# Turning the delta rule's outputs in 32 x 32 blocks on VectorE and placing the blocks by four loads, in a hybrid decoder layer

## The chip, the core and the metric

The kernel runs on one core of a Trainium2 chip. The metric is the device time of one execution in microseconds (us); lower is better. The program is built once, and its instructions stand in a fixed order on each engine: TensorE (PE), VectorE (DVE), ScalarE (ACT), GpSimd (POOL), and SyncE (SP), which issues most of the DMAs.

## What is computed

One decoder layer on 1024 tokens of 1024 features, in float32. After an RMS norm, one projection feeds two groups of four heads each: differential attention (group A) and a gated delta rule in chunks (group B). Their outputs are put side by side, projected, added to the input, and a squared-ReLU MLP of width 4096 follows.

```python
h = rms_norm(x, norm1_w); proj = h @ w_in
da_o = diff_attention(rms_norm(da_q), rms_norm(da_k), da_v, lam)      # 4 heads, values of 128
da_o = rms_norm(da_o, da_out_norm_w) * (1.0 - lam_init)
dn_o = gated_delta_rule(l2(conv_silu(q)), l2(conv_silu(k)), conv_silu(v), g, beta)
dn_o = rms_norm(dn_o, dn_out_norm_w) * silu(dn_z)                     # 4 heads of 128
x = x + concatenate([da_o, dn_o]) @ w_out
x = x + square(relu(rms_norm(x, norm2_w) @ w_up)) @ w_down
```

## The kernel before

Every large product is three matmuls of float32r parts: `hH` and `hL` hold the rounded value and the rest of the normed input, features on the partitions and tokens along the row. The order on TensorE is written out ahead of time by a planner, the class `Interleave` (L39): each stream of work is a generator with a priority, `flow.pe(ns)` moves the planned time on, `flow.chain(...)` gives the planned end of a chain on other engines, and `flow.hold(bank, t)` keeps a PSUM bank from being claimed before time t. The other engines' instructions are put in order by the framework's scheduler. The planner's times only set the order; on the chip every instruction waits for its own inputs.

The change lies between about 250 and 625 us, where these streams share TensorE:

- `scan` (L912) walks the eight chunks of 128 tokens of the delta rule. Its loads are `pka` (L920). `scan_out` (L966) makes a chunk's outputs: it loads `pkb` (L970) and `zgt` (L972), runs two sets of four matmuls (L980, L987), squares and sums on ScalarE (L994), and then a `scalar_tensor_tensor` for each head (L999) leaves the normed and gated rows, tokens on the partitions, in `oc`. GpSimd's queue stores them to `mixn_d` in DRAM (L1001).
- `da_units` (L1051) computes the queries, keys and values of the attention, two heads at a time (L1077 to L1079, 24 matmuls for one tile of 128 tokens). These matmuls are also what the planner fills gaps with. A finished tile of queries or keys goes on the list `late` with a due time; `da_turns` (L1030) takes it from there, turns it by two TensorE transposes (L1038, L1039) in a PSUM bank of the pool `px`, splits it and stores it to `qk_d` (L1044).
- `scores` (L1151) and `values` (L1232) are the attention, row of 128 queries by row, in the order head 0, head 1, and then heads 2 and 3 by turns from the last rows to the first. `scores` loads the keys `KS` (L1128) and the queries (L1143, L1144), multiplies (L1203, L1204), takes the maximum on VectorE (L1214) and the exponential on ScalarE (L1215). `values` turns the weights on TensorE (L1248, copied by L1250), multiplies by the values (L1260) into the bank `po`, copies the result to `om` (L1269), squares it into another part of the same bank (L1270) and scales it (L1274). Rows of heads 0 and 1 are stored to `mixa_d` by GpSimd's queue (L1276); for heads 2 and 3 the rows of one tile lie in `rows_of[tb]`, into whose first half the two stored heads are loaded (L1241).
- `mix_loads` (L1297) loads a stored tile of the delta rule's outputs into `mt` (L1305). `mixed` (L1308) calls `turn` (L1288) and through it `to_hT` (L293): four TensorE transposes into a `px` bank (L298), a rounding copy to `hH` (L303, ScalarE) and the rest to `hL` (L304, VectorE). It does so twice for each tile: for the four heads of the delta rule (`mt`) and for the four of the attention (`mx`).
- `outproj` (L1335) is the output projection from `hH` and `hL` (`half`, L1350 to L1352), followed for each tile by `norm2` (L1363): squares on ScalarE (L1370), the scale on VectorE (L1377) or ScalarE and GpSimd (L1379, L1380). `backs` (L1479) then turns the normed rows on TensorE (L298 for the first four tiles, which also keep a copy, L302; L1456 for the others).

The pool `px` has two PSUM banks for the query and key turns, the weights' turns, the `po` products and the `mixed` turns. SyncE's DMAs carry one of eight semaphores in rotation, so each also waits for the landing of the DMA eight places ahead of it. The MLP follows from 625 us to the end.

Of the kernel before, what the change touches and what calls it, by code (L numbers as in the profile page):

```python
# [18 lines left out]
P = 128  # L19
# [14 lines left out]
MIX_T = 5000.0  # L34
DMA_T = 2500.0
# [76 lines left out]
def vec(n, extra=0.0):  # L112
    return "V", 68.0 + 1.045 * n + extra
# [7 lines left out]
def tile_hymba_layer(  # L121
# [171 lines left out]
    def to_hT(src, tb, bank, k0=0, nk=KB, keep=None):  # L293
        sl = slice(tb * P, (tb + 1) * P)
        for g in range(0, nk, 4):
            ps = bank()
            for j in range(4):
                T.transpose(ps[:, j * P:(j + 1) * P], src[:, (g + j) * P:(g + j + 1) * P], ident)  # L298
            psv = ps.rearrange("p (k t) -> p k t", k=4)
            ks = slice(k0 + g, k0 + g + 4)  # L300
            if keep is not None:
                S.copy(keep, psv)  # L302
            S.copy(hH[:, ks, sl], psv)  # L303
            V.tensor_tensor(hL[:, ks, sl], psv, hH[:, ks, sl].bitcast(F32), ALU.subtract)  # L304
# [406 lines left out]

    def cols4(t, h, hf):
        return t[:, 8 * h + 4 * hf:8 * h + 4 * hf + 4]
# [252 lines left out]
    def scan_out(c, Sold, yy):  # L966
# [31 lines left out]
        for h in range(HEADS):  # L998
            V.scalar_tensor_tensor(oc[:, h * P:(h + 1) * P], oc[:, h * P:(h + 1) * P], f[:, h:h + 1],  # L999
                                   zgt[:, h * P:(h + 1) * P], ALU.mult, ALU.mult)  # L1000
# [4 lines left out]
        flow.chain(*[act(P, True)] * 4, vec(4), powr(4), vec(4), *[vec(P, 60)] * 4, start=t)  # L1005
# [45 lines left out]
    def da_units():  # L1051
# [12 lines left out]
        for i, (g, kind) in enumerate(todo):  # L1064
            (wh, wl), wt = w
            for j in range(NT):
# [17 lines left out]
                while len(late) > 2:  # L1084
                    yield flow.now + 50, None
# [7 lines left out]
                else:  # L1093
# [12 lines left out]
                    t = flow.chain(vec(4), powr(4), vec(256), start=t - flow.HOP)  # L1106
# [44 lines left out]
    def scores():  # L1151
        heads, npe, nsc = {}, 0, 0
        while state["da"] < 1:
            yield flow.now + 300, None
        heads[0] = load_head(0, ap), load_v(0, ap)
        q = load_q(*order[0])
        yield state["da_t"] + 3000, None
# [74 lines left out]
    def values():  # L1232
        for _ in order:
# [3 lines left out]
            if h == 2:  # L1237
                while "ax" not in pools or len(rows_of) + len([x for x in loads if not x[3]]) > 1:
                    yield flow.now + 50, None
                rows_of[tb] = pools["ax"].tile([P, 512], F32, tag="mx", name="mx", bufs=2)  # L1240
                nc.sync.dma_start(rows_of[tb][:, 0:256], mixa_d[tb])  # L1241
# [25 lines left out]
            sq = po[:, P:2 * P]  # L1267
# [6 lines left out]
            V.scalar_tensor_tensor(om, om, f, dawb, ALU.mult, ALU.mult)  # L1274
            if h < 2:
                nc.gpsimd.dma_start(mixa_d[tb, :, h * P:(h + 1) * P], om)  # L1276
            flow.pe((tb + 1) * MM)
            t = flow.chain(act(P))
            flow.hold(r, t)
# [6 lines left out]
    landed, hns = {}, {}  # L1286

# [9 lines left out]
    def mix_loads():  # L1297
        while not (pre and state["scan"]):
            yield flow.now + 200, None
        for i, t in enumerate(tiles):  # L1300
            while i >= 2 + state["mixed"]:
                yield flow.now + 50, None
            mt = pools["a2"].tile([P, 512], F32, tag="mt", name="mt", bufs=2)
            with tc.issue_after(newest["SP"].ins):
                nc.sync.dma_start(mt, mixn_d[t])  # L1305
            loads.append((mt, flow.now + MIX_T, t, 4))

    def mixed():  # L1308
        for i in range(2 * NT):
# [3 lines left out]
            x = min((x for x in loads if x[2] in over), key=lambda x: x[1])  # L1313
            r = yield from flow.bank("px")
            loads.remove(x)
            turn(r, *x)
            state["mixed"] += x[3] == 4
# [17 lines left out]
    def outproj():  # L1335
# [27 lines left out]
        def norm2(tb, pos):  # L1363
# [5 lines left out]
            for i in range(2):  # L1369
                S.activation(hn[i], accs[tb][:, 512 * i:512 * i + 512], AF.Square, accum_out=ss[:, i:i + 1])  # L1370
# [557 lines left out]
```

## Time and profile before

| | |
|---|---|
| median of 3 runs | 1233.85 us (1232.64 to 1236.31) |
| profiled execution: its own time | 1233.5 us |
| profiled execution: span from first to last instruction | 1231.8 us |
| granted TensorE clock, mean | 0.998 |
| PE busy | 1215.3 us, 99% |
| DVE busy | 829.9 us, 67% |
| ACT busy | 624.3 us, 51% |
| POOL busy | 151.3 us, 12% |

A row of a group reads: line, engine, operation, out<-in and shapes, count | busy us, mean ns of one | idle us of the engine before them and what ended it. In the list of waits, "PE a L1 <- DMA b: 2.8, 1, 2.8" says that PE stood idle ahead of line 1 until a transfer landed: in total, how often, and the longest. A view of one line gives durations as min/median/max in ns, and under a line that issues DMAs the time from issue to landing in us. In the timeline a row begins with its start in us and its length. A line number belongs to the kernel that the profile is of.

### The profile page before, as it was taken

The page shows a single profiled execution, that of the slowest core. Times are in us where ns is not written, and L with a number is a line of the kernel's source. Part 1 is how long each engine was busy: PE and PEld are TensorE (multiplying, and loading weights), DVE is VectorE, ACT ScalarE, POOL GpSimd, SP SyncE. Part 2 cuts the span into 40 slices and gives each one's busy share as a digit, 9 for nine tenths or more (in the row PEclk, how much of TensorE's full clock was granted, in tenths as well). Part 3 has the DMA queues.
Part 4 walks back from the last instruction along what each step waited for, and adds up shares of the span by engine and source line. Part 5 has one row for each costly group of instructions (what it writes and reads, how often), then busy time and mean ns, then how long its engine had stood idle before and what let it go on. Part 6 is the DMA issues. An engine that isn't in the chain of part 4 may idle for free.

```text
span 1231.8 us, 18793 instructions
## 1 busy us (share of the span) xinstructions
PE 1215.3 (99%) x6791; PEld 1052.0 (85%) x6791; DVE 829.9 (67%) x1534; ACT 624.3 (51%) x1249; POOL 151.3 (12%) x215
## 2 busy tenths in 40 slices
PE   9999999998999999999999999999999999999998
PEld 8978888898999998888888888888888888888886
DVE  6868797665647657776799544565569755777543
ACT  6587553344356555566766544454564333333330
POOL 2411110033434421001200000000000000000000
PEclk9999999999999999999999999999999999999999
DMA  9334654378648855223437433444479655423401
GB/s 351 103 111 119 167 163 86 78 244 240 223 146 246 241 162 159 84 74 109 157 120 257 171 129 145 171 171 154 154 244 386 229 178 184 162 103 103 137 35 69
DMA packets 155973, 202.12 MB, mean 164 GB/s; under 512 B 37688, under 2 KB 110952, under 8 KB 155880
## 3 DMA queue, kind: packets, MB, share of 16 engines
q1 hardware_dynamic: 151256, 187.28, 46.9%
q0 software_dynamic: 4480, 13.64, 2.9%
q8 instruction: 54, 0.88, 0.3%
q14 instruction: 39, 0.32, 0.1%
q10 hardware_dynamic: 144, 0.00, 0.0%
HBM read 135.86 MB, written 65.01 MB: 163 GB/s over the span
## 4 chain that ended last, share of the span: by engine, by line
PE 90%; DMA 3%; DVE 2%; ACT 2%; issue 1%; SPq 1%; POOL 1%; DVEq 0%; ACTq 0%; POOLq 0%
PE X L1527 5%; PE X L1526 5%; PE X L1525 5%; PE X L1825 4%; PE X L1823 4%; PE X L1824 4%; PE ps_dn L265 3%; PE ps_dn L267 3%; PE ps_dn L266 3%; PE ps_qk L1077 3%; PE ps_qk L1079 3%; PE ps_qk L1078 3%; PE Y L1525 3%; PE Y L1526 3%; PE Y L1527 3%; PE ps_o L1260 2%
## 5 line engine op out<-in xcount | busy, mean ns | idle before, releaser
L1443 ACT CAST hH<-ur 128x1024 fp32r<-128x1024 f32 x56 | 58.9, 1051 | 173.4 <-PE Y L1824 89.4
L1444 DVE TENSOR_TENSOR hL<-ur,hH 128x1024 fp32r<-128x1024 f32 x56 | 68.4, 1223 | 78.9 <-ACT hH L1443 78.8
L1077 PE MATMUL ps_qk<-wH,hH 128*128 128x256 f32 x384 | 115.1, 300 | 0.0
L1079 PE MATMUL ps_qk<-wH,hL 128*128 128x256 f32 x384 | 109.0, 284 | 0.0
L1078 PE MATMUL ps_qk<-wL,hH 128*128 128x256 f32 x384 | 108.9, 284 | 0.0
L1444 DVE TENSOR_TENSOR op<-raw,op 128x1024 fp32r<-128x1024 f32 x48 | 58.7, 1224 | 74.1 <-PE X L1526 41.1
L1823 PE MATMUL X<-hH 128*128 128x512 f32 x224 | 87.1, 389 | 0.0
L1824 PE MATMUL X<-hL,hH 128*128 128x512 f32 x224 | 87.1, 389 | 0.0
L1825 PE MATMUL X<-hH,hL 128*128 128x512 f32 x224 | 87.1, 389 | 0.0
L265 PE MATMUL ps_dn<-hH,wH 128*128 128x512 f32 x192 | 76.0, 396 | 0.2 <-ACT cp L679 0.2
L266 PE MATMUL ps_dn<-hL,wH 128*128 128x512 f32 x192 | 75.8, 395 | 0.0
L267 PE MATMUL ps_dn<-hH,wL 128*128 128x512 f32 x192 | 75.5, 394 | 0.0
L1077 PEld LDWEIGHTS ps_qk<-wH,hH 128*128 128x128 f32 x384 | 74.0, 193 | 0.5 <-DVE sn L1098 0.2
L1078 PEld LDWEIGHTS ps_qk<-wL,hH 128*128 128x128 f32 x384 | 74.0, 193 | 0.2
L1079 PEld LDWEIGHTS ps_qk<-wH,hL 128*128 128x128 f32 x384 | 73.6, 192 | 0.0
L1444 DVE TENSOR_TENSOR hL<-dw,hH 128x1024 fp32r<-128x1024 f32 x56 | 68.2, 1219 | 1.4 <-ACT hH L1443 1.4
L1443 ACT CAST op<-raw 128x1024 fp32r<-128x1024 f32 x48 | 50.4, 1051 | 35.7 <-PE Y L1527 19.9
L1443 ACT CAST hH<-dw 128x1024 fp32r<-128x1024 f32 x56 | 58.7, 1049 | 10.9 <-DMA dw<-in_w_down_dram 5.5
L1215 ACT ACTIVATE pexp<-pexp,mx 128x128 f32<-128x128 f32 (+7 forms) x64 | 49.7, 777 | 24.5 <-DVE mx L1214 24.1
L683 DVE SCALAR_TENSOR_TENSOR cy<-cp,pv,cy 128x512 f32<-128x512 f32 x72 | 53.7, 747 | 8.4 <-ACT cy L681 7.5
L1350 PE MATMUL ps_op<-wH,hH 128*128 128x512 f32 x128 | 53.0, 414 | 0.0
L1352 PE MATMUL ps_op<-wH,hL 128*128 128x512 f32 x128 | 50.3, 393 | 0.0
(374 smaller groups left out, 3424.2 us busy)
## 6 DMA issues: line engine op xcount, KB each, us to landing
ur<-ud SPq DMA_DIRECT2D x28, 1024.0 KB, 5.3
raw<-in_w_up_dram SPq DMA_DIRECT2D x32, 512.0 KB, 4.2
dw<-in_w_down_dram SPq DMA_DIRECT2D x32, 512.0 KB, 6.5
wraw<-in_w_units_dram SPq DMA_DIRECT2D x48, 256.0 KB, 3.6
qk_d<-qa POOLq DMA_DIRECT2D x32, 256.0 KB, 4.2
ud<-ua SPq DMA_DIRECT2D x16, 512.0 KB, 4.3
ud<-s SPq DMA_DIRECT2D x16, 512.0 KB, 2.7
pka<-park_d SPq DMA_DIRECT2D x32, 192.0 KB, 4.3
```

The lines of the kernel that those rows point to most:

```text
L265: T.matmul(ps, lh(k), rh(k), start=(k == 0), stop=False)
L266: T.matmul(ps, lh(k), rl(k), start=False, stop=False)
L267: T.matmul(ps, ll(k), rh(k), start=False, stop=(k == n - 1))
L1077: T.matmul(ps[:, :256], hH[:, k, sl], wh[:, k, :], start=(k == 0), stop=False)
L1078: T.matmul(ps[:, :256], hH[:, k, sl], wl[:, k, :], start=False, stop=False)
L1079: T.matmul(ps[:, :256], hL[:, k, sl], wh[:, k, :], start=False, stop=(k == KB - 1))
L1443: S.copy(dst[0], src)
L1444: V.tensor_tensor(dst[1], src, dst[0].bitcast(F32), ALU.subtract)
L1525: T.matmul(ps, op[0][:, k, cs], h[0][:, k, :], start=start and k == 0, stop=False, skip_group_check=True)
L1823: T.matmul(bank[t], v[0][:, j, sl], v[2][:, j], start=s0, stop=False, skip_group_check=True)
L1824: T.matmul(bank[t], v[0][:, j, sl], v[3][:, j], start=False, stop=False, skip_group_check=True)
L1825: T.matmul(bank[t], v[1][:, j, sl], v[2][:, j], start=False, stop=s1, skip_group_check=True)
```

## The change

- The delta rule's gated rows are written to `zgt`, and one VectorE `transpose` turns the 128 x 512 tile into `oc`: each 32 x 32 block is turned in its own place. The tile is stored to `mixn_d` in that form. `get_blocks` loads it back by four DMAs, one for each 32 partitions, which put each block's rows of 32 numbers (128 bytes) where the whole transpose has them.
- The rows of heads 0 and 1 are scaled into the third part of the `po` bank, turned in the same way into `om` and stored to `mixa_d`; `get_blocks` loads them with four DMAs as well. Their `po` bank is held until the block turn has read it.
- `mixed` therefore has no TensorE transposes for the delta rule's half of a tile (`settle`: the rounding copy and the rest, straight from SBUF), and two instead of four for the attention's half (`turn_last`).
- The squares of `values` go to a tile of their own, `osq2`, instead of the `po` bank.
- A query or key tile is due for its turn 1500 ns later by the plan (`TURN_T`), and one more may wait (`late > 3`). Head 0's keys are loaded 4500 ns later by the plan (`HEAD_T`), and the first scores come 6000 ns after that.
- For the last four tiles, `norm2`'s squares come, in ScalarE's order, behind the newest rounding copy of a kept tile (L303).

```diff
@@ -32,6 +32,8 @@
 MARGIN = 0.25
 SCAN_START = 18000.0
 MIX_T = 5000.0
+TURN_T = 1500.0
+HEAD_T = 4500.0
 DMA_T = 2500.0
 AHEAD = 2
 
@@ -300,7 +302,9 @@
             ks = slice(k0 + g, k0 + g + 4)
             if keep is not None:
                 S.copy(keep, psv)
-            S.copy(hH[:, ks, sl], psv)
+                newest["kept"] = S.copy(hH[:, ks, sl], psv)
+            else:
+                S.copy(hH[:, ks, sl], psv)
             V.tensor_tensor(hL[:, ks, sl], psv, hH[:, ks, sl].bitcast(F32), ALU.subtract)
 
     pctx = ctx.enter_context(ExitStack())
@@ -709,6 +713,13 @@
             nc.sync.dma_start(dst[:, s].rearrange("(b s) r -> s b r", s=32),
                               src[s].rearrange("s (b r) -> s b r", r=32))
 
+    def get_blocks(dst, src):
+
+        k = dst.shape[1] // P
+        src = src.rearrange("(a s) (k b r) -> b s k a r", s=32, k=k, r=32)
+        for b in range(4):
+            nc.sync.dma_start(dst[32 * b:32 * b + 32].rearrange("s (k a r) -> s k a r", k=k, r=32), src[b])
+
     def cols4(t, h, hf):
         return t[:, 8 * h + 4 * hf:8 * h + 4 * hf + 4]
 
@@ -996,13 +1007,14 @@
         rstd(f, so, 1.0 / P, EPS, sb, "oft", 4)
         V.tensor_tensor(f, f, rq[:, c::8], ALU.mult)
         for h in range(HEADS):
-            V.scalar_tensor_tensor(oc[:, h * P:(h + 1) * P], oc[:, h * P:(h + 1) * P], f[:, h:h + 1],
-                                   zgt[:, h * P:(h + 1) * P], ALU.mult, ALU.mult)
+            hs = slice(h * P, (h + 1) * P)
+            V.scalar_tensor_tensor(zgt[:, hs], oc[:, hs], f[:, h:h + 1], zgt[:, hs], ALU.mult, ALU.mult)
+        V.transpose(oc, zgt)
         nc.gpsimd.dma_start(mixn_d[c], oc)
         flow.pe(4 * MM)
         t = flow.chain(vec(512))
         flow.hold("pB", t)
-        flow.chain(*[act(P, True)] * 4, vec(4), powr(4), vec(4), *[vec(P, 60)] * 4, start=t)
+        flow.chain(*[act(P, True)] * 4, vec(4), powr(4), vec(4), *[vec(P, 60)] * 4, vec(512, 100), start=t)
         if c == NT - 1:
             s2ctx.close()
             spctx.close()
@@ -1081,7 +1093,7 @@
                         flow.pe(6 * TR)
                         if k < KB - 1:
                             yield wt[k // 2 + 1], None
-                while len(late) > 2:
+                while len(late) > 3:
                     yield flow.now + 50, None
                 qn = sd.tile([P, 256], F32, tag="qn", name="qn", bufs=4)
                 if kind == 2:
@@ -1103,7 +1115,7 @@
                     t = flow.chain(act(256))
                     flow.chain(act(256), start=t - flow.HOP)
                     freed[n % 2] = t = flow.chain(vec(256), start=t - flow.HOP)
-                    t = flow.chain(vec(4), powr(4), vec(256), start=t - flow.HOP)
+                    t = flow.chain(vec(4), powr(4), vec(256), start=t - flow.HOP) + TURN_T
                     late.append((g, kind, tb, qn, t))
                 quarters.block()
                 if i == len(todo) - 1:
@@ -1152,9 +1164,10 @@
         heads, npe, nsc = {}, 0, 0
         while state["da"] < 1:
             yield flow.now + 300, None
+        yield flow.now + HEAD_T, None
         heads[0] = load_head(0, ap), load_v(0, ap)
         q = load_q(*order[0])
-        yield state["da_t"] + 3000, None
+        yield flow.now + 6000, None
         for u, (h, tb) in enumerate(order):
             if u >= NT - 3 and 1 not in heads and state["scan"] or h == 1 and 1 not in heads:
 
@@ -1238,7 +1251,7 @@
                 while "ax" not in pools or len(rows_of) + len([x for x in loads if not x[3]]) > 1:
                     yield flow.now + 50, None
                 rows_of[tb] = pools["ax"].tile([P, 512], F32, tag="mx", name="mx", bufs=2)
-                nc.sync.dma_start(rows_of[tb][:, 0:256], mixa_d[tb])
+                get_blocks(rows_of[tb][:, 0:256], mixa_d[tb])
             ats = []
             for g in range(0, tb + 1, 4):
                 r = yield from flow.bank("px")
@@ -1264,18 +1277,22 @@
             else:
 
                 om = rows_of[tb][:, h * P:(h + 1) * P]
-            sq = po[:, P:2 * P]
+            sq = ap.tile([P, P], F32, tag="osq2", name="osq2", bufs=1)
             so = ap.tile([P, 1], F32, tag="so2", name="so2", bufs=2)
             S.copy(om, po[:, :P])
             S.activation(sq, om, AF.Square, scale=ri[:, 0:1], accum_out=so)
             f = ap.tile([P, 1], F32, tag="of2", name="of2", bufs=2)
             rstd(f, so, 1.0 / P, EPS, ap, "oft2", 1)
             V.tensor_tensor(f, f, ri[:, 0:1], ALU.mult)
-            V.scalar_tensor_tensor(om, om, f, dawb, ALU.mult, ALU.mult)
-            if h < 2:
-                nc.gpsimd.dma_start(mixa_d[tb, :, h * P:(h + 1) * P], om)
             flow.pe((tb + 1) * MM)
             t = flow.chain(act(P))
+            if h < 2:
+                V.scalar_tensor_tensor(po[:, 2 * P:3 * P], om, f, dawb, ALU.mult, ALU.mult)
+                V.transpose(om, po[:, 2 * P:3 * P])
+                nc.gpsimd.dma_start(mixa_d[tb, :, h * P:(h + 1) * P], om)
+                flow.hold(r, flow.chain(act(P, True), vec(1), powr(1), vec(1), vec(P, 60), vec(P, 60), start=t))
+                continue
+            V.scalar_tensor_tensor(om, om, f, dawb, ALU.mult, ALU.mult)
             flow.hold(r, t)
             t = flow.chain(act(P, True), vec(1), powr(1), vec(1), vec(P, 60), start=t)
             if h == 3:
@@ -1284,6 +1301,24 @@
 
     tiles = list(reversed(range(NT)))
     landed, hns = {}, {}
+
+    def settle(src, tb, ks, t=None):
+        sl = slice(tb * P, (tb + 1) * P)
+        sv = src.rearrange("p (k t) -> p k t", t=P)
+        S.copy(hH[:, ks, sl], sv)
+        V.tensor_tensor(hL[:, ks, sl], sv, hH[:, ks, sl].bitcast(F32), ALU.subtract)
+        n = P * (ks.stop - ks.start)
+        return flow.chain(act(n), vec(n), start=t)
+
+    def turn_last(r, src, t, tb):
+        settle(src[:, 0:256], tb, slice(0, 2))
+        ps = bank_tile(px, r, "ps_tr")
+        for j in (2, 3):
+            T.transpose(ps[:, j * P:(j + 1) * P], src[:, j * P:(j + 1) * P], ident)
+        flow.pe(2 * TR)
+        t = settle(ps[:, 256:512], tb, slice(2, 4))
+        flow.hold(r, t)
+        landed[tb, 0] = t
 
     def turn(r, src, t, tb, k0, keep=None):
         to_hT(src, tb, lambda: bank_tile(px, r, "ps_tr"), k0, 4, keep)
@@ -1302,7 +1337,7 @@
                 yield flow.now + 50, None
             mt = pools["a2"].tile([P, 512], F32, tag="mt", name="mt", bufs=2)
             with tc.issue_after(newest["SP"].ins):
-                nc.sync.dma_start(mt, mixn_d[t])
+                get_blocks(mt, mixn_d[t])
             loads.append((mt, flow.now + MIX_T, t, 4))
 
     def mixed():
@@ -1311,10 +1346,14 @@
             while not any(x[1] <= flow.now and x[2] in over for x in loads):
                 yield flow.now + 50, None
             x = min((x for x in loads if x[2] in over), key=lambda x: x[1])
+            if x[3] == 4:
+                loads.remove(x)
+                landed[x[2], 4] = settle(x[0], x[2], slice(4, 8))
+                state["mixed"] += 1
+                continue
             r = yield from flow.bank("px")
             loads.remove(x)
-            turn(r, *x)
-            state["mixed"] += x[3] == 4
+            turn_last(r, *x[:3])
         while not state["attn"]:
             yield flow.now + 50, None
         scctx.close()
@@ -1366,8 +1405,9 @@
             hn = [hn[:, 0:512], hn[:, 512:1024]]
             ss = laid("nss")
             nc.sync.dma_start(acc_d[tb], accs[tb])
-            for i in range(2):
-                S.activation(hn[i], accs[tb][:, 512 * i:512 * i + 512], AF.Square, accum_out=ss[:, i:i + 1])
+            with tc.issue_after(newest["kept"].ins) if pos >= 4 and "kept" in newest else ExitStack():
+                for i in range(2):
+                    S.activation(hn[i], accs[tb][:, 512 * i:512 * i + 512], AF.Square, accum_out=ss[:, i:i + 1])
             V.tensor_tensor(ss[:, 0:1], ss[:, 0:1], ss[:, 1:2], ALU.add)
             r = laid("nr")
             rstd(r, ss[:, 0:1], 1.0 / DM, EPS, None, "nrt", 1)
```

## The prediction

> **What bounds the kernel now.** I read the head of the page and its chain first.
>
> ```profile
> span 1231.8 us, 18793 instructions
> PE 1215.3 (99%) x6791; PEld 1052.0 (85%) x6791; DVE 829.9 (67%) x1534; ACT 624.3 (51%) x1249; POOL 151.3 (12%) x215
> ...
> PE 90%; DMA 3%; DVE 2%; ACT 2%; issue 1%; SPq 1%; POOL 1%; DVEq 0%; ACTq 0%; POOLq 0%
> ```
>
> TensorE is busy for all but 16.5 us of the span and carries 90% of the chain that ended last. A matmul that is taken away shortens the kernel by its place in the stream, unless its neighbours then wait for something else. The stretches come next.
>
> ```profile
> core 0: us, PE busy (x) PEld busy (x) DVE busy (x) ACT busy (x) POOL busy (x), PEclk, DMA share, GB/s
> 250.00:360.00 110.00, 105.41 (x884) 104.47 (x882) 63.82 (x194) 46.64 (x140) 42.05 (x55) 0.98 0.70 222
> 360.00:460.00 100.00, 98.18 (x798) 96.11 (x797) 65.24 (x198) 62.60 (x171) 42.70 (x62) 1.00 0.70 212
> 460.00:580.00 120.00, 118.86 (x710) 103.71 (x709) 89.28 (x242) 75.06 (x198) 14.34 (x26) 1.00 0.36 103
> ...
> 660.00:930.00 270.00, 270.00 (x1193) 223.57 (x1192) 163.12 (x143) 138.77 (x137) 0.00 (x0) 1.00 0.51 182
> ```
>
> The change lies in the first three. TensorE idles there for 4.6, 1.8 and 1.1 us, and no other engine is above 75%. The MLP has no idle time and is not touched. The clock is granted in full. TensorE's own list of waits names what can be won besides the matmuls:
>
> ```profile
> PE ps_o L980 <- DMA pkb<-park_d: 2.8, 1, 2.8
> PE ps_qkt L1038 <- DVE qn L1102: 1.8, 3, 1.0
> ...
> PE ps_qkt L1038 <- ACT ps_o L1270: 1.3, 2, 1.0
> ...
> PE ps_at L1248 <- ACT ps_o L1270: 0.8, 2, 0.7
> ...
> PE ps_sc L1204 <- DMA qb<-qk_d: 0.3, 1, 0.3
> ```
>
> **The transposes that go.** In the changed program's order there are 48 fewer TensorE instructions: all 32 turns of `mt` and half of the 32 of `mx`.
>
> ```profile
> L298 PE MATMUL ps_tr<-ident,mt 128*128 128x128 f32 x32 | 4.8, 272 | 0.0
> L298 PE MATMUL ps_tr<-ident,mx 128*128 128x128 f32 x32 | 4.8, 272 | 0.0
> ...
> 430.94 0.44 PE ps_tr L298 x4
> ```
>
> One matmul shows 272 ns, but they overlap: four take 0.44 us of the chain, 0.11 us each. 48 x 0.11 = **-5.3 us**, if what stood behind them is ready. Where they were the cover of another step they are worth nothing; that is a rival below.
>
> **What VectorE gets for it.** Eight turns of 128 x 512 and 16 of 128 x 128. Only the first size is in the trace, in another place:
>
> ```profile
> L864 DVE STREAM_TRANSPOSE kn<-cth x4: 670/709/717, 191.1 to 233.4; 128x512 f32<-128x512 f32 x4
> L1274 DVE SCALAR_TENSOR_TENSOR om<-om,of,dawb x16: 345/352/353, 374.5 to 497.0; 128x128 f32<-128x128 f32 x16
> ```
>
> 8 x 0.71 = 5.7 us. A small one lies between a quarter of the large one (0.18) and the scaling of the same tile (0.35): I take 0.25, so 16 x 0.25 = 4.0 us. The 9.7 us fall into the first two stretches and the start of the third, where VectorE idles for 46 + 35 us; the planner lets them in with 0.70 us a large turn, near the row. Behind a large turn wait the store to `mixn_d`, the next `zgt` load, and on VectorE whatever follows, at worst the next chunk's update. All of it has a chunk's time to come (8 chunks in about 100 us), so I take 0 on the path, and 8 x 0.71 = 5.7 us as the end if every large turn stood ahead of a step that TensorE awaits; below 0 it can't go, since nothing is removed from VectorE's chain here. The Trainium skill speaks against the choice of engine: "VectorE: DVE Perf Modes", Rules for kernel authors, has a 128 x 128 transpose go to TensorE if PSUM will do as its place. By that rule the 9.7 us of VectorE would buy 5.3 us of TensorE, a loss of 4.4 us, if the two engines' times weighed the same; the busy shares (67% against 99%) say they do not, and the sum goes by the shares.
>
> **The `po` bank.** A row of head 0 or 1 now holds its bank until the block turn has read it; before, until the squares were done.
>
> ```profile
> 484.32 1.72 PE L1260 MATMUL ps_o<-vt,at 128*128 128x128 f32 x14
> 486.08 0.27 ACT L1269 COPY om<-ps_o 128x128 f32<-128x128 f32 x1 [1.78 <-PE ps_o L1260]
> 486.68 0.19 ACT L1270 ACTIVATION_READ_ACCUMULATOR ps_o<-om,ri 128x1 f32 x1
> 489.37 0.35 DVE L1274 SCALAR_TENSOR_TENSOR om<-om,of,dawb 128x128 f32<-128x128 f32 x1
> ...
> 430.41 0.28 PE L1077 MATMUL ps_qk<-wH,hH 128*128 128x256 f32 x1
> 430.53 0.28 PE L1078 MATMUL ps_qk<-wL,hH 128*128 128x256 f32 x1
> ```
>
> Here the bank was held 0.8 us past the product (486.04 to 486.87); with scaling and turn it is 489.72 + 0.25, so 3.9 us. In the changed order between 28 and 57 matmuls stand from the end of such a product to the first claim on what its turn releases. The shortest covers of the unit stage have 32, mostly of the form that starts every 0.12 us (430.41, 430.53): 3.8 us. So two or three of 16 rows come out about even, and a late row costs a few tenths. For heads 2 and 3 the squares no longer touch the bank, which then is free 0.6 us earlier. Of the 2.1 us of waits on L1270 I take **-1.4**, with ends of -2.1 and +1.5 (16 rows late by 0.1).
>
> **Later keys.** The 1.8 us of waits for `qn` are at most 1.0 us each, and the turns now stand 1.5 us later by the plan: **-1.8**, at worst 0. The 2.8 us wait for `pkb` comes from SyncE's order:
>
> ```profile
> 279.82 0.33 PE L1038 MATMUL ps_qkt<-ident,qn 128*128 128x128 f32 x1 [1.03 <-DVE qn L1102]
> ...
> 282.91 3.86 DMA qk_d<-qa
> ...
> 286.84 0.69 SPq L1128
> ...
> 289.66 7.24 DMA pkb<-park_d
> 296.94 1.35 PE ps_o L980 x6
> ```
>
> The four `KS` loads wait for the last key tile's store, and the `pkb` loads are queued behind them: 17.1 us from the eighth key turn to the matmul that needs them. That order stays (`pka`, `KS`, a `zgt`, `KS`, `pkb`). What changes is the distance on TensorE: 97 instructions from turn to matmul before, 147 after, which at 0.11 to 0.12 us is 11 against 17 us, and the loads now wait for slots that come free only after the store has landed. So the stall of 2.8 us should go: **-2.8**, at worst 0. Two loads of queries and the chunk's `pka` are queued behind too; their matmuls come later still. The first scores stand 26 instructions later, after more of the unit matmuls that follow one another anyway: 0, and were the fillers short at the end of the units, the 26 x 0.12 = 3 us that the give-back below allows for.
>
> **The block loads.** 64 DMAs instead of 16 on SyncE, in pieces of 128 bytes. The same form was stored (L709) and loaded (L812) elsewhere:
>
> ```profile
> L709 SPq DMA_DIRECT2D park_d<-kn x32: 302/494/552, 185.5 to 235.6; - x32
> DMA to landing us min/median/max: 1.8/2.0/3.7
> ...
> L812 SPq DMA_DIRECT2D gb<-fsg_d x32: 303/430/1105, 193.4 to 229.1; - x32
> DMA to landing us min/median/max: 1.6/1.7/3.0
> ...
> L1305 SPq DMA_DIRECT2D mt<-mixn_d x8: 320/327/585, 417.1 to 450.3; - x8
> DMA to landing us min/median/max: 2.7/3.4/4.0
> ```
>
> A tile now takes 4 x 0.49 us to issue and 2.0 us for the last piece: 3.5 us after the first issue, as the single load did. The rounding copy (`settle`) stands in ScalarE's order and waits there for the last piece, where before TensorE's turn stood between; behind it are the copies that TensorE needs for the weights' products. Six tiles of the attention's half load only when a buffer comes free, with 1.5 to 2.6 us of TensorE's stream, 2.3 on most, before ScalarE's order comes to the copy. Its last piece is issued after 3 x 0.43 = 1.3 us and lands 2.0 later, so ScalarE is blocked about 1 us, most of it covered by projection matmuls. And the query loads behind stand 1.3 us later at SyncE, where 0.3 us of waiting shows already. I take **+1.0**; ends 0 and +3.
>
> **The rest.** The squares behind the bank copies and the split of the copies into two halves of 256 change ScalarE's and VectorE's order under the last projection matmuls: 0, with -0.3 to +0.5. The planner's new order as a whole has waits that this trace cannot show. The named ones that go make 6.0 us, and I give a quarter back: **+1.5**, ends 0 and +3.
>
> **Sum.** -5.3 - 1.8 - 2.8 - 1.4 + 1.0 + 1.5 = -8.8 us. The profiled execution took 1233.5 us, 1.7 more than its span of 1231.8, and lies 0.35 below the median. Against the median, 1233.85 - 8.8 = **1225.0 us**. What a measurement can tell from no change is 0.3%, 3.7 us.
>
> **Rivals.** (a) *Only the transposes pay.* The waits come back at other places, as the `po` banks' longer hold and ScalarE's block waits could do: 1233.85 - 5.3 = 1228.5. For it: 6.0 us of waits in 360 us of a planned order are few, and a new order rarely has none. Against: each wait has its own remedy with a margin in the order.
>
> (b) *The transposes were cover.* In 460 to 580 us their places lay between a weights' copy and the product that needs it; without them TensorE waits there for ScalarE, and the 5.3 us come back with most of the waits: 1232.5, no difference. For it: the x4 groups stand next to L1260 in the old order. Against: projection matmuls fill the same gaps, and 32 of the 48 lay in the unit stage, which has fillers of its own.
>
> (c) *The block loads come late: slower.* Place: ScalarE's `settle` copies of the six attention tiles. With a last piece that lands p after its issue, ScalarE is blocked 1.3 + p - 2.3 us, of which four matmuls of the projection (270.00 / 1193 = 0.226 us each) cover 0.9: next to nothing at p = 2.0, 3.1 us at p = 5.0, six times 18.6 us, so 1225.0 - 1.0 + 18.6 = 1242.6. The gain is gone from p = 3.5 (6 x 1.6 = 9.8), beside the longest store piece (3.7), and from 4.2 it is slower by 0.3%. The Trainium skill has a rule of this kind: "DMA: Bandwidth & Descriptors", Specifications, wants at least 512 bytes for line rate and says that smaller pieces are read, modified and written. So far the traces bear it out little: the 128-byte rows land in 1.7 to 2.0 us, no later than the row loads' 3.4.
>
> That the change does not do what it says is excluded by the built order for the 48 transposes; for the waits it is rival (a).
>
> **Chances.** Forecast 0.54, (a) 0.24, (b) 0.13, (c) 0.07, and 0.02 for waits beyond those named. Faster than 1230.1: forecast and (a) with the better edge of the rest, 0.79; within 0.3%: 0.13; slower: 0.08. The low end takes every better end (-5.3 - 1.8 - 2.8 - 2.1 - 0.3 = -12.3) and half of the waits that the busy time hides: of the three like matmuls of a step the first takes longest,
>
> ```profile
> L1077 PE MATMUL ps_qk<-wH,hH 128*128 128x256 f32 x384 | 115.1, 300 | 0.0
> L1079 PE MATMUL ps_qk<-wH,hL 128*128 128x256 f32 x384 | 109.0, 284 | 0.0
> ```
>
> by 16 ns, 384 times: 6 us. 1233.85 - 12.3 - 3 = 1218. The high end takes in (a) with its worse ends and (b): 1234; (c) stays out.
>
> **What would show it.** Right: the `ps_tr` rows of L298's place count 48 fewer turns; the time from 250 us to the MLP's start is about 9 us shorter and the rest equal; TensorE waits for `pkb`, `qn` and the squares for less than 1 us each. Wrong: TensorE waits for block turns for more than 2 us in all; ScalarE's copies to `hH` from `mt` or `mx` idle before a DMA for more than 1 us each; the stretch is as long as before although the turns are gone, with new waits before L1260.

## The result

The changed kernel takes 1228.05 us (median of 6 runs, 1226.96 to 1231.73), the kernel before 1234.44 us in the same runs (6, 1232.64 to 1236.31). The ratio is 0.9958, 95% interval 0.9943 to 0.9973: 5.2 us less, between 3.3 and 7.0. The medians lie 6.4 us apart, since two of the changed kernel's six runs took 1231.3 and 1231.7 us and the other four 1227.0 to 1228.4. The forecast was 1225.0 us in a range of 1218 to 1234. The sign and the range hold; the value lies 3 us too low (3.6 by the ratio), half a microsecond from rival (a), *only the transposes pay* (1228.5).

The profiled execution took 1227.74 us with a span of 1226.0. First the head of the page of the changed kernel, then its stretches in the columns of the prediction:

```profile
span 1226.0 us, 18798 instructions
PE 1208.2 (99%) x6743; PEld 1045.9 (85%) x6743; DVE 836.9 (68%) x1566; ACT 624.0 (51%) x1257; POOL 151.9 (12%) x215
```

```profile
250.00:360.00 110.00, 108.56 (x941) 107.94 (x942) 69.92 (x206) 48.02 (x147) 42.99 (x55) 1.00 0.72 226
360.00:460.00 100.00, 95.95 (x750) 93.41 (x750) 69.42 (x212) 63.34 (x174) 41.45 (x61) 0.98 0.79 217
460.00:580.00 120.00, 117.55 (x689) 101.66 (x688) 88.70 (x248) 74.36 (x204) 15.15 (x27) 1.00 0.38 101
660.00:930.00 270.00, 270.00 (x1193) 223.64 (x1192) 163.70 (x144) 137.33 (x136) 0.00 (x0) 1.00 0.51 184
```

TensorE has 48 matmuls and 7.1 us of busy time less, but 17.8 us idle in place of 16.5. Idle time in the first stretch fell from 4.6 to 1.4 us, and rose from 1.8 to 4.1 and from 1.1 to 2.4 us in the next two. The list of TensorE's waits shows what came:

```profile
PE ps_o L1273 <- DVE qa L1055: 2.3, 1, 2.3
...
PE ps_at L1261 <- ACT at L1263: 1.3, 2, 1.1
PE ps_qkt L1050 <- DVE om L1291: 1.0, 1, 1.0
PE ps_o L1273 <- ACT at L1263: 1.0, 1, 1.0
...
PE ps_qkt L1050 <- ACT at L1263: 0.7, 1, 0.7
...
PE ps_qk L1089 <- DVE sn L1110: 0.7, 1, 0.7
PE ps_qkt L1050 <- DVE qn L1114: 0.7, 1, 0.7
```

The 2.8 us for `pkb` and the 2.1 us for the squares are gone and the 1.8 us for `qn` are 0.7. That makes 6.0 us, the sum that was forecast, but by luck: the squares gave 0.7 more than their term and `qn` 0.7 less. In their place stand 7.0 us: all rows above but the last. Two of them stand next to each other. The timeline of the changed kernel there (start, length, engine, line, output from input; in brackets the idle time before):

```profile
384.36 0.35 DVE L1290 SCALAR_TENSOR_TENSOR ps_o<-om,of,dawb 128x128 f32<-128x128 f32 x1
...
384.75 0.32 DVE L1291 STREAM_TRANSPOSE om<-ps_o 128x128 f32<-128x128 f32 x1
...
385.21 0.30 PE L1050 MATMUL ps_qkt<-ident,qn 128*128 128x128 f32 x1 [1.04 <-DVE om L1291]
...
386.17 0.27 PE L1050 MATMUL ps_qkt<-ident,qn 128*128 128x128 f32 x1
...
388.34 0.48 ACT L1263 COPY at<-ps_at 128x384 f32<-128x384 f32 x1 [2.21 <-PE ps_at L1261]
...
390.04 0.93 ACT L1228 ACTIVATE pexp<-pexp,mx 128x768 f32<-128x768 f32 x1 [1.22 <-DVE mx L1227]
...
390.98 0.45 ACT L1054 ACTIVATE qa<-ps_qkt,pv 128x256 fp32r<-128x256 f32 x1
...
391.46 0.48 DVE L1055 SCALAR_TENSOR_TENSOR qa<-ps_qkt,pv,qa 128x256 fp32r<-128x256 f32 x1 [0.58 <-ACT qa L1054]
...
392.00 1.01 PE L1273 MATMUL ps_o<-vt,at 128*128 128x128 f32 x3 [2.28 <-DVE qa L1055]
```

At 385.21 TensorE wants the bank that the small block turn (L1291) reads last: the longer hold of `po` that the prediction weighed. The second wait has nothing to do with blocks. The key turn of 386.17 ends at 386.5, but in ScalarE's order its copy (L1054) stands behind an `at` copy and an exponential, and runs at 390.98; the product needs the bank that this copy and L1055 free. The three rows for `at` copies, 3.0 us, come from ScalarE's order as well. The wait of 1.0 us that ends at 574.09 is for the copy at 573.80, which runs behind the squares of `norm2` and a rounding copy:

```profile
571.88 0.61 ACT L1410 ACTIVATE hn<-acc 128x512 f32<-128x512 f32 x1
...
572.50 0.61 ACT L1410 ACTIVATE hn<-acc 128x512 f32<-128x512 f32 x1
...
573.11 0.39 ACT L1308 CAST hH<-mx 128x256 fp32r<-128x256 f32 x1
...
573.80 0.24 ACT L1263 COPY at<-ps_at 128x128 f32<-128x128 f32 x1
```

To see where time went over all kernels, three marks were read from each trace: the start of the first unit matmul, of the first TensorE instruction behind the last unit matmul, and of the MLP's first matmul. In us:

| kernel | ratio to before, 95% | median | units | attention and projection | MLP to the end |
|---|---|---|---|---|---|
| before | 1 | 1234.4 | 231.9 | 156.1 | 617.5 |
| changed | 0.9958 (0.9943 to 0.9973) | 1228.05 | 227.0 | 155.7 | 617.1 |
| e1 turns out, old order | 0.9993 (0.9983 to 1.0003) | 1234.36 | 231.1 | 156.3 | 618.7 |
| e2 plan only | 1.0007 (0.9999 to 1.0016) | 1234.47 | 232.1 | 157.3 | 617.8 |
| e3 plan undone | 1.0037 (1.0022 to 1.0052) | 1237.77 | 227.8 | 165.7 | 618.6 |
| e4 row loads | 0.9951 (0.9939 to 0.9963) | 1227.72 | 224.8 | 156.0 | 617.2 |
| e5 plan undone, row loads | 1.0002 (0.9993 to 1.0011) | 1233.65 | 226.3 | 159.5 | 617.6 |
| e6 delta half only | 1.0013 (1.0004 to 1.0023) | 1235.83 | 230.8 | 158.9 | 618.6 |
| e7 key turns not later | 1.0073 (1.0061 to 1.0085) | 1242.81 | 231.2 | 164.4 | 618.6 |
| e8 first keys not later | 0.9984 (0.9975 to 0.9992) | 1231.51 | 229.3 | 155.4 | 617.1 |
| e9 plan, turns out | 0.9986 (0.9975 to 0.9997) | 1232.18 | 228.1 | 156.2 | 619.3 |
| e10 first keys 1000 ns earlier | 1.0065 (1.0052 to 1.0077) | 1242.24 | 230.9 | 163.2 | 617.5 |
| e11 key turns 500 ns later | 0.9940 (0.9929 to 0.9952) | 1226.97 | 226.3 | 155.9 | 617.3 |
| e12 more buffers | 0.9946 (0.9932 to 0.9959) | 1226.18 | 223.4 | 156.7 | 617.2 |

The stages are those of one profiled execution each. One differs from the next by a few microseconds even in the same order: e12 gains 2.2 us on e11 between 300 and 320 us, where both run the same instructions in the same order.

The change's gain lies in the units: 4.9 of 5.8 us of span. 28 of the 48 turns lay there; at 0.107 us each, the price that e1 gives below, they make 3.0, and shorter waits and closer matmuls gave the other 1.9. In the next stage 20 turns went (2.1 us), and 0.3 us was won.

### The profile page after: what moved, and what is told of

Read it like the earlier page. It is cut to its first block, busy times and chain, and to the rows that moved or that the text cites. A ratio compares the mean times of both kernels' runs of the same rounds, so it can differ in the third digit from the quotient of the medians.

```text
span 1226.0 us, 18798 instructions
## 1 busy us (share of the span) xinstructions
PE 1208.2 (99%) x6743; PEld 1045.9 (85%) x6743; DVE 836.9 (68%) x1566; ACT 624.0 (51%) x1257; POOL 151.9 (12%) x215
## 4 chain that ended last, share of the span: by engine, by line
PE 91%; ACT 3%; DVE 2%; DMA 2%; SPq 1%; issue 1%; POOL 0%; DVEq 0%; ACTq 0%
PE X L1567 5%; PE X L1565 5%; PE X L1566 5%; PE X L1864 4%; PE X L1863 4%; PE X L1865 4%; PE ps_dn L267 3%; PE ps_qk L1089 3%; PE ps_dn L269 3%; PE ps_dn L268 3%; PE ps_qk L1090 3%; PE ps_qk L1091 3%; PE Y L1567 3%; PE Y L1565 3%; PE Y L1566 3%; PE ps_o L1273 3%
```

## The experiments

**e1, the turns alone.** Before's order of everything else is kept.

```diff
-        to_hT(src, tb, lambda: bank_tile(px, r, "ps_tr"), k0, 4, keep)
+        if keep is not None:
+            to_hT(src, tb, lambda: bank_tile(px, r, "ps_tr"), k0, 4, keep)
+        else:
...
+            n = 4 if k0 else 2
+            sv = src.rearrange("p (k t) -> p k t", t=P)
+            parts = [(slice(k0, k0 + n), sv[:, 0:n])]
+            if n == 2:
...
+                for j in (2, 3):
+                    T.transpose(ps[:, j * P:(j + 1) * P], src[:, j * P:(j + 1) * P], ident)
...
+            for ks, v in parts:
+                S.copy(hH[:, ks, sl], v)
...
```

> The kernel before with the 48 TensorE turns left out and every other TensorE instruction in its old order: the rounding copies read the loaded rows of the delta rule's half and of heads 0 and 1 unturned, so the layout of hT is not the reference's there. The forecast's first term (48 x 0.11 us, nothing waits in their place): 5.3 us less than before, 1229.1 us, with TensorE's idle time between 250 and 580 us still about 7.5 us. The rival that the turns were cover: TensorE's idle time grows by what its busy time loses, no difference, 1233 to 1235 us.

1234.36 us: no difference. Since the order is the same, the starts of matching TensorE instructions can be subtracted. An instruction that stood at 430.05 us in before starts at 431.55 in e1, 1.50 later through waits further ahead; the one at 432.02, behind the first group of turns left out, starts at 433.09, 1.07 later. So four turns are worth 0.43 us, 0.107 each. Every other group of four without a new wait behind it shows 0.43 as well, and every pair of turns 0.21 or 0.22. The price was right. But what is gained is lost again: 1.2 us at 436.30, for a bank that a key turn's copy (L1043) had not freed, and later behind these waits of e1:

```profile
PE ps_at L1248 <- ACT ps_o L1270: 1.2, 3, 0.7
...
PE ps_o L1260 <- DVE qa L1043: 1.0, 1, 1.0
PE Y L1539 <- DVE ua L1579: 1.0, 1, 1.0
...
PE ps_tr L298 <- POOL hn L1394: 0.9, 1, 0.9
```

Before has 0.8 for the first row, 0.4 for the last, and neither of the others. So rival (b) holds in the old order: there the turns were cover.

**e2, the plan alone, and e9, the plan with the turns out.**

```diff
+TURN_T = 1500.0
+HEAD_T = 4500.0
...
-                while len(late) > 2:
+                while len(late) > 3:
...
-                    t = flow.chain(vec(4), powr(4), vec(256), start=t - flow.HOP)
+                    t = flow.chain(vec(4), powr(4), vec(256), start=t - flow.HOP) + TURN_T
...
+        yield flow.now + HEAD_T, None
...
-        yield state["da_t"] + 3000, None
+        yield flow.now + 6000, None
```

e9 adds the edit of e1 to it.

> The kernel before with the four planning changes alone (key turns 1500 ns later, first keys 4500 ns later, first scores 6000 ns after their loads, three key tiles allowed to wait). The forecast's term: the waits for qn (1.8 us) and pkb (2.8 us) go, 4.6 us less, 1229.8 us. The rival that waits come back at other places: TensorE's idle time stays at 16 to 18 us, 1233 to 1236 us.

> The kernel before with the four planning changes and without the 48 TensorE turns, all other TensorE instructions in the order of the plan-only run; the rounding copies read unturned rows, so the layout of hT is not the reference's in those rows. Theory (the turns pay in full once the keys stand later): 48 x 0.107 = 5.1 us below the plan-only run, 1229.3 us. Rival (the turns cover other steps in this order as well): less than 2 us below it, 1232.5 to 1234.5 us, with new TensorE waits behind the places of the turns.

e2: 1234.47 us, no difference; its waits are

```profile
PE ps_sc L1206 <- DMA qa<-qk_d: 1.5, 2, 1.3
PE ps_o L982 <- DMA pkb<-park_d: 1.5, 2, 1.1
PE ps_sc L1207 <- DMA qb<-qk_d: 1.2, 2, 0.7
PE ps_at L1251 <- ACT ps_o L1273: 1.2, 5, 0.4
```

`qn` is gone from the list, as forecast; `pkb` fell by half only, and query loads came in. Between 250 and 355 us TensorE idles 1.8 us in place of 4.6, and in the next 100 us 4.3 in place of 1.8: moved, not won. e9 is 2.6 us faster than e2 by the ratios, half of the turns' 5.1. Neither expectation is met in full: turns pay more in this order than in the old one, and not all. By the ratios e9 is still 3.5 us slower than the changed kernel, which leaves out the same turns. What lies between the two (the squares' own tile, the blocks, the place of `norm2`'s squares, the order that the planner writes) is not taken apart further.

**e3, the plan undone in the changed kernel, and e5, the same with row loads.** e3 takes the lines of e2's diff back; e5 also has

```diff
-                get_blocks(rows_of[tb][:, 0:256], mixa_d[tb])
+                nc.sync.dma_start(rows_of[tb][:, 0:256], mixa_d[tb])
...
-                get_blocks(mt, mixn_d[t])
+                nc.sync.dma_start(mt, mixn_d[t])
```

> The changed kernel with the four planning changes undone. The forecast's term: the waits for qn and pkb are back, 4.6 us more than the changed kernel, 1232.7 us. The rival (the planner gives back what it wins): within 1.5 us of the changed kernel, 1226.5 to 1229.5 us, with other waits in the list of waits.

> The changed kernel with the four planning changes undone, as in the run before, and one plain load in place of each four block loads in the same order (the layout of hT is then not the reference's in those rows). Theory: without the planning changes the block loads stand on SyncE right ahead of query loads, and TensorE's waits for qa and qb (4.2 us in the list of waits) are theirs: they fall under 1.5 us, and the time falls by 3 to 4.5 us, to 1233.3 to 1234.8 us. Rival: the order as a whole costs the time, the block loads nothing, as in the changed kernel: within 1 us of 1237.8 us.

e3: 1237.77 us, 9.7 above the changed kernel, twice the forecast's term, and slower than before. Its units are near the changed kernel's (227.8 us); the loss is in the attention and projection, 165.7 against 155.7. The timeline of e3 there, SyncE and TensorE:

```profile
567.24 2.56 SPq L721 DMA_DIRECT2D mx<-mixa_d  x4
...
569.90 0.56 SPq L1155 DMA_DIRECT2D qa<-qk_d  x1
570.55 0.54 SPq L1156 DMA_DIRECT2D qb<-qk_d  x1
571.14 0.59 SPq L1155 DMA_DIRECT2D qa<-qk_d  x1
...
571.78 0.59 SPq L1156 DMA_DIRECT2D qb<-qk_d  x1
...
573.49 0.30 PE L1215 MATMUL ps_sc<-KS,qa 128*128 128x128 f32 x1 [1.65 <-DVE cf L1237]
574.26 0.30 PE L1216 MATMUL ps_sc<-KS,qb 128*128 128x128 f32 x1 [0.48 <-DMA qb<-qk_d]
```

Four block loads keep SyncE for 2.56 us, and the query loads of the scores stand right behind. The first wait is put down to `cf`, which no score reads; what the matmul needs is the `qa` load issued at 571.14, 2.35 us before, as the next one needs the `qb` load issued at 571.78, 2.48 us before. e5, in the same order, issues one load of 0.53 us there (at 563.50) and takes 1233.65 us: 4.1 less, within the expectation. The waits for `qa` and `qb` fall from 4.2 to 2.4 us, less far than expected. All waits ahead of score matmuls in this stage, under whatever name, fall from 7.8 to 3.3 us. The stage is 159.5 us, 6.2 shorter, of which 1.7 are a dip of the clock at 574.6 us that e5 does not have (last section). So without the planning changes the block loads cost some 4 us, through the time of issue.

**e4, row loads in the changed kernel.** The edit of e5 on the changed kernel.

> The changed kernel with one plain load in place of each four block loads, in the same order; the 32 x 32 blocks stay where they are, so the layout of hT is not the reference's in those rows. The forecast's term for the block loads (+1.0 us): 1227.0 us, and ScalarE's idle time before the copies from mx falls from 7.4 us to about 5. If the block loads are what gave the rest of the forecast back: 1224 to 1225 us with fewer TensorE waits at the at copies. If they cost nothing: 1228 us.

1227.72 us; stage 156.0 against 155.7. That is 0.3 us less than the changed kernel by the medians and 0.9 by the ratios, and the intervals overlap: no cost of the block loads is seen in this order, but the 1 us of the forecast is not excluded. In the two traces, which have the same order, matching instructions of e4 gain 1.8 us between 220 us and the MLP, and 1.45 of them are a dip of the clock that e4 does not have (last section); 0.4 are left. The expected fall of ScalarE's idle time did not come:

```profile
ACT hH L1308 <- DMA mx<-mixa_d: 7.8, 6, 2.4
```

It was 7.4 us with the blocks, so it is not the splitting into pieces that makes these copies wait. The rows of the changed kernel's block loads: their time on SyncE (ns, shortest, median and longest), then their size and median us to landing; and of VectorE's turns:

```profile
L721 SPq DMA_DIRECT2D mt<-mixn_d x32: 557/634/1646, 403.4 to 449.3; - x32
L721 SPq DMA_DIRECT2D mx<-mixa_d x32: 558/611/620, 500.3 to 570.4; - x32
```

```profile
mt<-mixn_d SPq DMA_DIRECT2D x32, 64.0 KB, 3.1
mx<-mixa_d SPq DMA_DIRECT2D x32, 32.0 KB, 2.1
```

```profile
L1012 DVE STREAM_TRANSPOSE oc<-zgt x8: 701/706/711, 269.6 to 358.5; 128x512 f32<-128x512 f32 x8
...
L1291 DVE STREAM_TRANSPOSE om<-ps_o x16: 298/316/317, 371.5 to 497.2; 128x128 f32<-128x128 f32 x16
```

Row loads in e5 land after 3.4 us (`mt`) and 2.0 (`mx`), the loads in pieces of 128 bytes after 3.1 and 2.1: a single load does not land later. But a tile takes four issues of 0.61 to 0.63 us, and counted from the first issue the last quarter of an `mt` tile lands after 5.6 us (median of the six that the trace shows), the row load of e4 after 3.1 (of five).

**e6, only the delta rule's half in blocks.** The rows of heads 0 and 1 are loaded plainly and turned by TensorE as before; plan, squares and the rest as changed.

```diff
-                get_blocks(rows_of[tb][:, 0:256], mixa_d[tb])
+                nc.sync.dma_start(rows_of[tb][:, 0:256], mixa_d[tb])
...
+            V.scalar_tensor_tensor(om, om, f, dawb, ALU.mult, ALU.mult)
             if h < 2:
-                V.scalar_tensor_tensor(po[:, 2 * P:3 * P], om, f, dawb, ALU.mult, ALU.mult)
-                V.transpose(om, po[:, 2 * P:3 * P])
...
-            turn_last(r, *x[:3])
+            turn(r, *x)
```

> The changed kernel with the rows of heads 0 and 1 turned by TensorE as before (16 turns back, the bank of the product free after its copy, no small block turns); the delta rule's half stays in blocks and the plan stays. Theory of single prices: 16 x 0.107 = 1.7 us more for the turns and 1.0 less for the wait on the block turn, 1228.7 us. Rival (the order decides, not the parts): more than 1.5 us away from that, on either side, with waits at new places.

1235.83 us, 7 above the sum of single prices: the rival. In the profiled execution, at 1238.93 us the slowest of its twelve, two waits for `qa` loads, at 395.61 and 459.74 us, make 7.2 us. Both are SyncE's: the queries of the first stand behind loads of `x` rows, those of the second behind the eight block loads of two `mt` tiles. Neither is of the part taken back.

**e7, e8, e10 and e11, one planned distance each.** TURN_T = 0; HEAD_T = 0; HEAD_T = 3500; TURN_T = 2000.

> The changed kernel with the key turns no longer planned 1500 ns later; all else as changed. The forecast's term: the waits for qn are back, 1.8 us more, 1229.8 us. Rival (waits only move): qn waits up by 1 us or more, but the time within 1 us of 1228.0, or off by more than 3 us through waits that have nothing to do with qn.

> The changed kernel with the first key loads no longer planned 4500 ns later; all else as changed. The forecast's term: the wait for pkb is back, 2.8 us more, 1230.8 us. Rival (waits only move): pkb waits up by 1 us or more and the 2.3 us wait at 392 us gone, the time within 1 us of 1228.0 us.

> The changed kernel with the first key loads planned 3500 instead of 4500 ns later; nothing else is edited, and the planner writes another order. Theory (the planner's order as a whole sets some microseconds, and no single wait does): more than 1.5 us away from 1228.0 us, on either side, with waits that have nothing to do with the first keys. Rival (each planned distance is a margin that acts smoothly): between the 1231.5 us of 0 ns and the 1228.0 us of 4500 ns, 1228.3 to 1229.3 us.

> The changed kernel with the key turns planned 2000 instead of 1500 ns later; nothing else is edited, and the planner writes another order. Theory (the planner's order sets some microseconds): more than 1.5 us away from 1228.0 us, on either side. Rival (margins act smoothly): the waits for qn fall from 0.7 us to 0, the time is 0 to 0.7 us lower.

1242.81, 1231.51, 1242.24 and 1226.97 us. HEAD_T at 0, 3500 and 4500 ns gives 1231.5, 1242.2 and 1228.05: not a margin that acts smoothly. TURN_T at 0 does bring the `qn` waits back (2.9 us), but the loss is some 14 us, so e7's rival holds. e8 costs 3.2 us by the ratios, near the forecast's 2.8, yet not by `pkb`, whose wait does not come back; it has one wait of 4.6 us at 365 us, for a score bank that VectorE reads late (L1227).

What sets the large steps: behind the units the planner writes one of two orders of TensorE. The changed kernel, e4, e8, e11 and e12 have the very same one (870 instructions up to the MLP), and this stage takes 155.4 to 156.7 us in all five, with at most 0.4 us of waits ahead of its score matmuls. e3, e5, e7 and e10 have the other (in e7 three projection matmuls stand elsewhere), with 163.2 to 165.7 us and 5.4 to 7.8 us of such waits for the block loads, and 159.5 us and 3.3 for the row loads of e5. That is 7.5 to 8.7 of the 14 us in e7 and e10; some 4 more lie in their units. The first order puts the score matmuls far enough behind their query loads that SyncE's 2.56 us fit in; the second does not. Which of the two comes out hangs on 1000 ns of a planned distance two hundred microseconds earlier: HEAD_T at 0 and 4500 ns gives the first, at 3500 ns the second. e11 lies 1.1 us (medians) to 2.2 us (ratios) below the changed kernel, and the intervals overlap, so its time decides nothing. Its list of waits has no `qn`, but the wait at the turn near 280 us is 1.0 us there, put down to `rnt`; a step on `qn` ends 0.15 us before the turn starts, as in the changed kernel.

**e12, more buffers for the block loads**, on e11, TensorE's order unchanged:

```diff
-                get_blocks(rows_of[tb][:, 0:256], mixa_d[tb])
+                own = pools["a2"].tile([P, 512], F32, tag="mt", name="mt", bufs=2) if tb % 2 else rows_of[tb]
+                halves[tb] = own[:, 0:256]
+                get_blocks(halves[tb], mixa_d[tb])
...
-        settle(src[:, 0:256], tb, slice(0, 2))
+        settle(halves[tb], tb, slice(0, 2))
```

> The kernel of the run with key turns planned 2000 ns later, its TensorE order kept; the blocks of heads 0 and 1 of every second row tile are loaded into the two mt buffers, which are free by then, so that a block load waits four tiles back for its buffer and not two. The forecast's term (+1.0 us for ScalarE, which stands for the last piece): ScalarE's idle time before the copies from mx falls from 8.5 us to under 3, the TensorE wait of 1.0 us at the copies near 574 us goes, and the time falls by about 1 us, to 1226.0 us. Rival (that idle time of ScalarE is covered by projection matmuls, as the run with row loads has it): the idle time falls as well, the time stays within 0.5 us of 1227.0 us.

1226.18 us against e11's 1226.97, 0.8 less; by the ratios it is 0.7 more, and the intervals overlap (0.9932 to 0.9959 and 0.9929 to 0.9952). The time decides nothing. ScalarE's waits before the copies, in the changed kernel, in e11 and in e12:

```profile
ACT hH L1308 <- DMA mx<-mixa_d: 7.4, 6, 2.3
```

```profile
ACT hH L1308 <- DMA mx<-mixa_d: 8.5, 6, 2.7
```

```profile
ACT hH L1310 <- DMA mt<-mixa_d: 3.6, 3, 1.4
```

Five microseconds of ScalarE's waiting went, and the stage did not get shorter (156.7 after 155.9). TensorE's wait at the copies near 574 us did not go either: 1.0 us in e11, 1.4 in e12.

```profile
PE ps_o L1275 <- ACT at L1265: 1.4, 1, 1.4
```

So the traces speak for the rival: this waiting is covered. Both e11 and e12 beat the kernel before; that either beats the changed kernel is not shown.

## Why the prediction was right in sign and 3 us too low

*The transposes, -5.3.* Right in price: 0.107 us each, 5.1 in all, by e1; 28 of them lay in the units, not 32. Wrong in that it stood as a term of its own: it pays nothing in the old order (e1), half with the new plan (e9), and with the block turns, the loads and the plan together the result is as large as the term by luck: it is a net of larger amounts.

*VectorE's turns, 0.* Right. A large one takes 0.706 us, a small one 0.316, not 0.25; VectorE is busy 7.0 us more, and no wait of TensorE names L1012. The rule of the Trainium skill against this engine ("VectorE: DVE Perf Modes", Rules for kernel authors) shows no loss here, with VectorE at 68%; no run puts the large turns alone back on TensorE.

*The `po` bank, -1.4.* The squares' 2.1 us went; a wait of 1.0 on the small turn came. Near enough: -1.1, in this order. In others the waits for the small turn are 2.0 to 3.1 us (e7, e10, e11, e12).

*Later keys, -1.8 and -2.8.* This step failed. The `qn` waits do follow TURN_T from 0 to 1500 ns (2.9 and 4.0 us in e7 and e3 without it, 0.7 with it), but not beyond (e11). But `pkb` does not follow HEAD_T (e8), and in e2, where this step stands alone, what it wins before 355 us is given back after. The prediction counted waits that end as time won.

*The block loads, +1.0.* Their size in the changed kernel is 0.3 to 0.9 us in e4, not told apart from 0 or from the term. The tile was to be complete 3.5 us after its first issue, as with the row load; an `mt` tile takes 5.6 against 3.1. The mechanism was looked for on ScalarE, whose waiting is covered (e12); where the loads do cost, some 4 us in e3, it is the time of issue on SyncE ahead of the queries, to which the prediction gave one sentence. The landing of a piece, from which rival (c) was to decide, shows no delay (3.1 and 2.1 us against 3.4 and 2.0); in that rival's sum 6 x 1.6 is 9.6, not 9.8, which changes nothing.

*The rest, 0.* The wait of 1.0 us at 574.09 stands behind `norm2`'s squares in ScalarE's order and is larger than the end of +0.5 that the term had. No run takes back the squares' place or the tile `osq2` alone, so what they give or cost is not shown.

*The give-back, +1.5.* The mis-sized term: the waits that came make 7.0 us. Against the 6.0 us that went, the waits as a whole net +1.0, near the 1.3 us by which TensorE's idle time grew. The turns' 5.1 less these 1.3 make 3.8 of the 5.8 us of span; the other 2.0 are spread over the spacing of all other matmuls, under 1 us in each group, and no run isolates them. The case for waits that come back was in the prediction as rival (a), at 0.24; the runs with other planned distances show that 1.5 us with an end of +3 was too narrow for it, since a new order moved the time between -1 and +14 us.

*What would show it.* 48 turns fewer: yes. A stretch 9 us shorter: no, 5.2 from the first unit matmul to the MLP (387.9 to 382.7). `pkb`, `qn` and the squares under 1 us each: yes. Of the signs of being wrong one came: before the copies from `mx` ScalarE idled for 7.4 us in 6, 1.2 each, which cost nothing that e4 or e12 can show. The waits for block turns stayed at 1.0 us, under the 2 named.

## What to carry to other kernels

Where a planner writes the order of an engine that is busy 99% of the time, a wait that ends is not time won: look for what is late next, and run the edit in two or three neighbouring plans before its price is believed, since here a planned distance moved by 500 to 1500 ns was worth up to 14 us. An edit's own price is found by keeping the order and subtracting the starts of matching instructions. When one load is split into four, count its issue time on the queue against the loads behind it, and three issues more until the tile is complete.

## What the runs showed of the hardware

A wait of TensorE can have a second price. The granted clock (third number from the right) falls in the windows around or behind its end, here before, the changed kernel, e6, and then e4, which has the same order and the same 2.3 us wait as the changed kernel:

```profile
295.00:300.00 5.00, 3.06 (x15) 2.94 (x16) 1.82 (x8) 0.00 (x0) 0.16 (x1) 0.78 0.86 284
300.00:305.00 5.00, 5.00 (x40) 5.00 (x40) 2.78 (x8) 2.22 (x5) 2.19 (x3) 0.88 0.64 201
```

```profile
390.00:395.00 5.00, 3.00 (x14) 3.00 (x15) 2.92 (x8) 3.52 (x9) 0.79 (x2) 0.68 1.04 348
395.00:400.00 5.00, 5.00 (x38) 4.85 (x38) 4.03 (x12) 3.07 (x8) 2.42 (x4) 0.98 0.62 188
```

```profile
395.00:400.00 5.00, 4.39 (x21) 4.34 (x22) 3.09 (x10) 0.95 (x2) 1.15 (x3) 0.66 0.69 222
```

```profile
390.00:395.00 5.00, 2.71 (x21) 2.39 (x20) 3.63 (x8) 3.12 (x10) 0.54 (x1) 1.00 1.05 366
395.00:400.00 5.00, 5.00 (x38) 4.84 (x38) 4.28 (x14) 3.54 (x9) 2.76 (x4) 1.00 0.80 228
```

(0.22 + 0.12) x 5 us, (0.32 + 0.02) x 5 and 0.34 x 5 all make 1.7 us of clock, and so does each of the other dips seen between 240 and 640 us: in every one the trace's clock record has 0.5 for 3.41 us, from 0.6 us before to 1.4 us after the end of a wait. e4 has none, and its matching instructions gain 1.45 us on the changed kernel's between 392 and 400 us. So the `pkb` wait of 2.8 us in before cost up to 4.5, and the new wait at 392 us up to 4.0. The prediction read the clock as granted in full, though the first of its stretches shows 0.98, and priced both sides without it. The runs show a price too, if a smaller one: of the 78 runs of the kernel before that were timed along with the experiments, the 29 with a granted clock of 1.000 average 1233.4 us and the 28 with 0.998 1234.5. The Trainium skill ("TensorE: Matmul & The Clock Gate", What's actually happening) has the clock at half in windows of 3.4 us that run freely. From this figure one such window costs an estimated 1.7 us, which agrees with the dips. It asks for about 3.4 us of idle time; here 2.3 us were enough in one execution and not in another, and in e2 a wait of 1.0 and one of 0.5 us, 1 us apart, were followed by the same dip.
